# Copying four quadrants of a 256 MB matrix: DMAs of 64 rows from the four quadrants in turn, in place of DMAs of 512 rows

## Chip, cores and metric

One core of one Trainium2 chip. The metric is the device time of one execution in microseconds (us). Three calls of experiments follow the first comparison; each ran on one chip (the record numbers them 5, 15 and 5) and shares its own runs of the kernel before. Kernels are compared only within the same rounds.

## The reference

```python
def setup_inputs():
    return {"x": np.random.randn(8192, 8192).astype(np.float32)}

def reference(x):
    return np.fft.ifftshift(x)      # swaps the quadrants crosswise
```

With an even size this exchanges quadrants of 4096 x 4096: upper left with lower right, upper right with lower left. A row of a quadrant is 16 KB in one piece; the whole matrix has rows of 32 KB.

## The kernel before

No engine computes. SP (`nc.sync`) and ACT (`nc.scalar`) each issue 16 DMAs from main memory to main memory. A DMA takes every eighth row of one quadrant: 512 rows, 256 KB apart, 8 MB. The two queues always copy diagonal quadrants, so that reads and writes of left and right halves balance.

```python
STEP = 8
...
    dims = [[STEP * C, hr // STEP], [1, hc]]
    for c in range(STEP):
        for col in (0, hc):
            for eng, r0, h in ((nc.sync, 0, col), (nc.scalar, hr, hc - col)):
                eng.dma_start(
                    out=bass.AP(out.tensor, out.offset + (r0 + c) * C + h, dims),
                    in_=bass.AP(x.tensor, x.offset + (hr - r0 + c) * C + hc - h, dims),
                )
```

## Time and profile before

| | before |
|---|---|
| time, median of the 6 runs beside the change | 822.26 us (821.98 to 822.82) |
| copied | 268.4 MB, 327 GB/s |
| read and written in main memory | 654 GB/s |
| 16 KB packet: quickest (all but 22 of 16384 take at least this), median, mean | 611, 773, 801 ns |
| DMAs, completion writes (4 bytes each, by which an engine reports that its part of a DMA is done) | 32, 512 |

The prediction below shows the busy lines, the queues and the rate by stretch. One more view: how long the issuing instruction itself took. This is the view of the output tensor; the columns are least, median and longest duration in ns, then the first and last start in us.

```profile
L33 ACTq DMA_DIRECT2D out_dram<-in_x_dram x16: 518/42177/48098, 0.7 to 618.8; - x16
L33 SPq DMA_DIRECT2D out_dram<-in_x_dram x16: 511/41599/47782, 0.7 to 613.7; - x16
```

The shortest issue takes 0.51 us. The median of 42 us is not work. As I read it, the instruction stands until the queue has room for the last of its rows, while the engines work on the rows ahead of it; the trace does not name what it waits for. The engines' busy share is 1.00 meanwhile, so it costs nothing here.

### The profile page before, as it was taken

How to read it: one execution, taken by the hardware profiler on the slowest of the kernel's cores; microseconds unless marked ns; L12 is line 12 of the kernel's file. 1: busy time of each engine (PE TensorE's matmuls, PEld its weight loads, DVE VectorE, ACT ScalarE, POOL GpSimd, SP SyncE). 2: the span in 40 equal slices, each digit the busy share in tenths (PEclk: the TensorE clock that was granted, in tenths of full speed). 3: DMA queues.
4: the chain of work that ended last, by engine and by line, in shares of the span. 5: the costliest groups of instructions: out<-in, count | busy, mean ns of one | idle time of the engine just before them, and what ended most of it. 6: DMA issues, size and time to landing. Idle time of an engine off the chain costs nothing. (4 is left out here: it accounts for less than half of the span.)

```text
span 821.3 us, 77 instructions
## 1 busy us (share of the span) xinstructions
POOL 0.2 (0%) x4
## 2 busy tenths in 40 slices
POOL 0000000000000000000000000000000000000000
DMA  9999999999999999999999999999999999999998
GB/s 304 325 328 333 326 325 330 321 329 330 325 330 330 327 328 333 329 330 330 328 328 327 334 325 330 326 326 328 331 329 330 326 332 326 328 324 333 326 328 298
DMA packets 16896, 268.44 MB, mean 327 GB/s; under 512 B 512, under 2 KB 512, under 8 KB 512
## 3 DMA queue, kind: packets, MB, share of 16 engines
q1 hardware_dynamic: 8448, 134.22, 50.2%
q10 hardware_dynamic: 8448, 134.22, 49.7%
HBM read 268.44 MB, written 268.44 MB: 654 GB/s over the span
## 5 line engine op out<-in xcount | busy, mean ns | idle before, releaser
L51 POOL MEMSET const-bfloat16-1.0<- 128x1 bf16 x1 | 0.1, 103 | 0.0
L51 POOL MEMSET const-uint8-127<- 128x1 uint8 x1 | 0.1, 102 | 0.0
L51 POOL MEMSET const-float32-0.0<- 128x1 f32 x1 | 0.1, 99 | 0.2 <-issue 0.2
L51 POOL MEMSET const-float32-1.0<- 128x1 f32 x1 | 0.1, 99 | 0.0
## 6 DMA issues: line engine op xcount, KB each, us to landing
out_dram<-in_x_dram ACTq DMA_DIRECT2D x16, 8192.0 KB, 204.3
out_dram<-in_x_dram SPq DMA_DIRECT2D x16, 8192.0 KB, 204.1
```

What stands on the lines that cost most here:

```text
L51: nc = _bacc.Bacc("TRN2", target_bir_lowering=False, num_devices=1)
```

## The change

The change alters which rows are in flight at one time: shorter DMAs, engines closer together, and all four quadrants within a short time rather than two. Each DMA is cut to 64 rows (1 MB), and the second pair of quadrants changes queues, so that SP writes both left quadrants and ACT both right ones.

```diff
 STEP = 8
+PARTS = 8
...
-    dims = [[STEP * C, hr // STEP], [1, hc]]
+    n = hr // STEP // PARTS
+    dims = [[STEP * C, n], [1, hc]]
     for c in range(STEP):
-        for col in (0, hc):
-            for eng, r0, h in ((nc.sync, 0, col), (nc.scalar, hr, hc - col)):
+        for part in range(PARTS):
+            row = c + part * n * STEP
+            for eng, r0, h in (
+                (nc.sync, 0, 0),
+                (nc.scalar, hr, hc),
+                (nc.sync, hr, 0),
+                (nc.scalar, 0, hc),
+            ):
                 eng.dma_start(
-                    out=bass.AP(out.tensor, out.offset + (r0 + c) * C + h, dims),
-                    in_=bass.AP(x.tensor, x.offset + (hr - r0 + c) * C + hc - h, dims),
+                    out=bass.AP(out.tensor, out.offset + (r0 + row) * C + h, dims),
+                    in_=bass.AP(x.tensor, x.offset + (hr - r0 + row) * C + hc - h, dims),
                 )
```

## The prediction

> **What bounds the kernel now.** The program computes nothing: it copies four quadrants of 4096 x 4096 float32 (64 MB each) from one place in memory to another, so I started with the busy line of the whole span, then the queues, then the issues, then what the issuing engine waits for, and last the rate in separate stretches.
>
> The busy lines and the queues of the page (one digit is a fortieth of the span, GB/s is what was copied in it):
>
> ```profile
> DMA  9999999999999999999999999999999999999998
> GB/s 304 325 328 333 326 325 330 321 329 330 325 330 330 327 328 333 329 330 330 328 328 327 334 325 330 326 326 328 331 329 330 326 332 326 328 324 333 326 328 298
> DMA packets 16896, 268.44 MB, mean 327 GB/s; under 512 B 512, under 2 KB 512, under 8 KB 512
> ...
> q1 hardware_dynamic: 8448, 134.22, 50.2%
> q10 hardware_dynamic: 8448, 134.22, 49.7%
> HBM read 268.44 MB, written 268.44 MB: 654 GB/s over the span
> ```
>
> The 16 DMA engines are busy from start to end; only the first and last slices are lower. The two queues share them evenly (50.2% and 49.7%). 16896 packets are 16384 rows of 16 KB plus 512 tiny ones, which are the completion writes: 32 DMAs times 16 engines. A byte copied is read once and written once, so memory carries 654 GB/s.
>
> Is "busy" a full engine, or one that waits for memory? The packet records of the trace say: a 16 KB packet takes 611 ns at its quickest and about a quarter take that, the median is 773 ns, the mean 801 ns. 16384 B / 611 ns is 26.8 GB/s, times 16 engines 429 GB/s, which would be 268.44 MB / 429 = 626 us. The mean, 1024 packets per engine times 0.801 us = 820 us, is the whole span. So a packet is on average 31% slower than an engine can go, and what slows it is common to all. The 16 completion writes of each DMA land within 0.6 to 1.3 us of each other, even at its end: no engine is ahead of the rest. That fits one saturated common resource, memory, and not a slow engine or queue.
>
> Issues, and the issuing engine's waits:
>
> ```profile
> out_dram<-in_x_dram ACTq DMA_DIRECT2D x16, 8192.0 KB, 204.3
> out_dram<-in_x_dram SPq DMA_DIRECT2D x16, 8192.0 KB, 204.1
> ...
> SPq L62 <- DMA out_dram<-in_x_dram: 167.2, 2, 118.8
> SPq L33 <- DMA out_dram<-in_x_dram: 133.8, 12, 50.6
> ```
>
> A DMA of 8 MB at half of 327 GB/s takes 51.3 us; it lands 204 us after its issue, so four are in flight per queue. SP waits 12 times = 16 - 4: it may issue the next when the one four back has landed. This wait costs nothing, since three others are still queued.
>
> Last, the rate by stretch, each stretch holding one pair of DMAs or two:
>
> ```profile
> 2.00:53.00 51.00, 0.00 (x0) 1.00 1.00 329
> 53.00:104.00 51.00, 0.00 (x0) 1.00 1.00 329
> 104.00:155.00 51.00, 0.00 (x0) 1.00 1.01 328
> 155.00:206.00 51.00, 0.00 (x0) 1.00 1.01 326
> 206.00:308.00 102.00, 0.00 (x0) 1.00 1.00 328
> 410.00:512.00 102.00, 0.00 (x0) 1.00 1.00 328
> 614.00:716.00 102.00, 0.00 (x0) 1.00 1.01 329
> ```
>
> The last column is GB/s. It stays between 326 and 329 whichever row phase (one of eight) and column half is being copied. Sorting the packets by their place within a DMA (rows 0 to 31 of an engine, 256 KB apart) I also found no pattern beyond the scatter: even and odd rows both 798 to 805 ns. The rate does not care which of these address bits are set.
>
> **What the Trainium skill says.** (1) "HBM Reference", Specifications (TRN2): about 716 GB/s for the memory that two cores share, here used by one. The trace's 654 GB/s is 91% of it, with reads and writes mixed. (2) "DMA: Bandwidth & Descriptors", Issuing engines are not separate DMA queues: DMAs issued from several engines run on the same 16 DMA engines and interleave, so choosing who issues saves only issue time. The 50.2% and 49.7% agree. (3) Same page, section on why a DMA increments its semaphore by 16: a DMA is split over the largest k up to 16 that divides its slowest dimension, and each engine used ends with its own completion write. 512 tiny packets for 32 DMAs agree with k = 16; 64 rows also give 16, four rows each. (4) Same page, Latency and other measured facts, row on HBM row pitch at large powers of two: copies lose rate as the pitch grows, 207 GB/s at 512 KiB, 164 at 2 MiB, 103 at 4 MiB, against 214 padded; it calls the mechanism an inference. The trace before has 327 GB/s at a 256 KB pitch, so those sizes do not carry over.
>
> **The change, part by part.**
>
> Removed: nothing of the data. The same 16384 packets of 16 KB, same source and destination pairs, 1024 per engine. The floor of 626 us and memory's 537 MB stay.
>
> Added, issues: 256 DMAs in place of 32, 128 per queue. When the queue had room an issue took 0.51 to 0.62 us in the trace; 128 x 0.6 = 77 us per queue, beside 820 us of data. One DMA of 1 MB at 163.5 GB/s per queue takes 6.4 us, ten times its issue. Not on the path.
>
> Added, completion writes: 256 x 16 = 4096 in place of 512, so 224 more per engine. The records give 9 ns for each: 224 x 9 ns = 2.0 us. An upper figure: the trace has 8.7 us in which only 15 engines were busy; put wholly on the 512 writes that is 17 ns more each, so 224 x 26 ns = 5.8 us. Where memory is the limit, the other engines can use that gap, so I take +2 us.
>
> Changed, depth: four DMAs in flight per queue are now 4 MB rather than 32 MB, per engine 4 x 4 = 16 packets per queue. After a landing the next must be issued (0.6 us) and reach the engines: the first packet in the trace starts 1.4 us after its issue started. Meanwhile 3 x 6.4 = 19 us of work is queued. A gap needs engines to drift apart by some 12 packets of a queue; the trace shows 1.3 us at most, under two packets. Cost 0.
>
> Changed, order: rows handled at one time. If each engine takes consecutive rows (32 before, 4 after), engines were 32 x 256 KB = 8 MB apart and become 1 MB apart; a queue alternates between two quadrants each 6.4 us, not each 51 us. At any moment SP still copies one quadrant and ACT the diagonal one, so the mix of column halves read and written stays. The stretches above show no dependence on address bits from 16 KB (column half) up to 4 MB (row within an engine's share), so I expect little, but the bits which differ between engines change from 8 MB upward to 1 MB upward, and no record before tests that. I give it -4 us, with a wide spread.
>
> Changed, ends: the start (1.4 us to the first packet) is as before. q10 ends 2 us after q1 in the landings; finer DMAs may save about half, 1 us, lost in the rest.
>
> Sum: 822.3 + 2 (completions) + 0 (issue, depth) - 4 (order) = 820 us.
>
> **Rivals.**
>
> A. Memory conflicts fall, because engines no longer walk 8 MB apart. For: the skill's pitch table (if its engines hold eight rows each, 512 KiB is 4 MB between engines and 2 MiB is 16 MB, a loss of 3% and 23%, and 8 MB lies between); packets scatter from 611 to 1826 ns. Against: 654 is already 91% of 716 GB/s. Even all 716 would be 536.9 MB / 716 = 750 us; an estimate of 94%, 673 GB/s, gives 798 us. Time 790 to 805 us.
>
> B. Conflicts grow: four engines' rows now fall where one engine's fell, and each queue jumps between quadrants every four rows. For: the same table shows that pitch can matter a lot. Against: the flat stretches. 3 to 5% fewer GB/s would be 845 to 865 us.
>
> C. The shallow queue runs dry, because a new DMA waits for the slowest engine of the one four back. For: 124 such waits per queue in place of 12. Against: 19 us queued against 2 us of refill. If each wait leaked 0.2 us on both queues together it would be 25 us, 847 us; the DMA share would fall below 0.97.
>
> **Range and chances.** The known terms are worth +2 to +6 us, the end effects 1 us; all the width comes from A, B and C. A's limit is near, since memory is at 91%, so the lower end is 795; B or C of moderate size give the upper end, 848. 2% is 16.4 us: below 806 is faster, which needs 667 GB/s or more over the span, a rate that single slices reach (334 copied, 668 moved) but no 51 us stretch holds. I give it 0.22. Slower needs B or C at more than 16 us: 0.18. Same: 0.60.
>
> **What would show it.** Right: 20480 packets with 4096 under 512 B; some 25.6 us (4 x 6.4) from issue to landing; SP waiting 124 times, each under 7 us; DMA share 1.00 in the middle; 325 to 331 GB/s in every stretch; a mean packet near 800 ns. A would show the mean packet below 785 ns, with more packets at 611. B would show DMA share 1.00 and a mean packet above 815 ns. C would show a share below 1.00 with packets unchanged or quicker. The prediction is wrong if memory's rate depends on how far apart the engines' rows lie, the one thing the trace before cannot show.

## The result

The changed kernel takes 821.96 us (median of 6 runs, 821.5 to 822.85), before 822.26 us in the same rounds. The ratio is 0.9997, 95% interval 0.9984 to 1.001. Ratios here are the mean time of one kernel's runs over that of the other's of the same rounds, so not quite the ratio of the medians quoted.

The changed kernel's busy lines and queues, from its page:

```profile
DMA  9999999999999999999999999999999999999998
GB/s 302 328 328 331 327 328 329 328 325 331 329 328 329 330 329 331 323 331 332 326 325 329 327 329 323 328 331 326 331 331 327 335 323 333 331 331 327 327 328 295
DMA packets 20482, 268.47 MB, mean 327 GB/s; under 512 B 4096, under 2 KB 4096, under 8 KB 4096
...
q1 hardware_dynamic: 10240, 134.23, 50.1%
q10 hardware_dynamic: 10240, 134.23, 49.7%
...
HBM read 268.44 MB, written 268.44 MB: 654 GB/s over the span
```

The same rates as before, slice by slice, with eight times the completion writes. Two packets over the expected 20480 are instruction fetches.

Its issues, with the median us from issue to landing last, then what SP waited for (us in total, times, longest), then the issue durations in ns:

```profile
out_dram<-in_x_dram ACTq DMA_DIRECT2D x128, 1024.0 KB, 25.5
out_dram<-in_x_dram SPq DMA_DIRECT2D x128, 1024.0 KB, 25.5
```

```profile
SPq L40 <- DMA out_dram<-in_x_dram: 728.5, 124, 8.3
```

```profile
L40 SPq DMA_DIRECT2D out_dram<-in_x_dram x128: 511/511/832, 0.7 to 797.0; - x128
```

SP now waits 728 us in place of 134, in 124 places. Looked at alone this would be a serious finding, yet nothing became slower: the time moved from "the issue stands in a full queue" (42 us each, before) to "the issue waits for the DMA four back" (5.9 us on average). By that count the queue always held three more DMAs.

The changed kernel's rate by stretch, last column GB/s, to set against the same stretches in the prediction:

```profile
2.00:53.00 51.00, 0.00 (x0) 1.00 1.00 330
53.00:104.00 51.00, 0.00 (x0) 1.00 1.00 330
104.00:155.00 51.00, 0.00 (x0) 1.00 1.00 328
206.00:308.00 102.00, 0.00 (x0) 1.00 1.00 329
410.00:512.00 102.00, 0.00 (x0) 1.00 1.01 327
614.00:716.00 102.00, 0.00 (x0) 1.00 1.01 330
```

The packet records show where the small known cost went. Per engine, all 16 KB packets together took 820.3 us before and 816.2 us after, 4.0 us less (of the unrounded sums); the completion writes took 0.3 us before and 2.3 us after, 2.0 us more; and time in which an engine did nothing (from the number of packets under way at each moment, the first and last 10 us left out) went from 0.5 to 2.2 us. What the engines lost in one place the packets gained in another. That is what one expects if a shared limit sets the pace, and it is what the experiments test.

### The profile page after: what moved, and what is told of

Read it like the earlier page. It is cut to its first block, busy times and chain, and to the rows that moved or that the text cites. A ratio compares the mean times of both kernels' runs of the same rounds, so it can differ in the third digit from the quotient of the medians. Undisturbed runs are those within 1.5% of the kernel's fastest.

```text
span 820.7 us, 301 instructions
## 1 busy us (share of the span) xinstructions
POOL 0.2 (0%) x4
## 2 busy tenths in 40 slices
DMA packets 20482, 268.47 MB, mean 327 GB/s; under 512 B 4096, under 2 KB 4096, under 8 KB 4096
## 6 DMA issues: line engine op xcount, KB each, us to landing
out_dram<-in_x_dram ACTq DMA_DIRECT2D x128, 1024.0 KB, 25.5
out_dram<-in_x_dram SPq DMA_DIRECT2D x128, 1024.0 KB, 25.5
```

## The experiments

Theory M: one resource that all engines share is full, and it cares neither for the order of the rows, nor for their distance, nor for the number of DMAs. Rivals: X, the two halves of the change have effects that cancel; E, each engine is slowed by itself; A, memory conflicts depend on addresses and the two kernels happen to be alike; C, the queue runs dry; S, completion writes come on top. And what is the resource: H, main memory read and written together, or F, the way through the engines?

### order_only and size_only: the two halves of the change

`order_only` is the changed kernel with this edit:

```diff
-PARTS = 8
+    PARTS = 1
```

`size_only` is the changed kernel with the quadrants on the queues as before:

```diff
-                (nc.sync, hr, 0),
-                (nc.scalar, 0, hc),
+                (nc.sync, 0, hc),
+                (nc.scalar, hr, 0),
```

> Half of the change alone: DMAs of 512 rows as before, quadrants in turn as after (SP takes both left quadrants of the output, ACT both right ones). Theory M (one shared resource is full at 327 GB/s copied and does not care for the order): 822 us, within 0.3%. Rival X (two effects of the change that cancel): over 0.5% off, and size_only off by as much the other way.

> The other half alone: 64 rows per DMA as after, quadrants on the queues as before. Theory M: 822 to 824 us (224 more completion writes per engine, at most 2 us). Rival X: over 0.5% off and opposite to order_only.

Measured: 824.53 and 824.57 us, before on that chip 824.07 us; ratios 1.0001 (0.9986 to 1.0016) and 1.0005 (0.999 to 1.002). Neither half does anything, so nothing cancels: X falls. The distance between the engines belongs to size_only; order_only leaves it as before, since its DMAs keep their rows. That distance and completion writes do not cancel inside size_only is shown by apart1m_rows (that distance, no more writes) and rows16 (still more writes) below.

### engines15 and engines12: fewer DMA engines

The rows per DMA are chosen so that 15 or 12 is the largest number of engines that divides them; the remaining rows of each quadrant go in one last DMA on 16.

```diff
-    dims = [[STEP * C, hr // STEP], [1, hc]]
-    for c in range(STEP):
+    n = 492        # 12 engines; 510 for 15
+    main = [[STEP * C, n], [1, hc]]
+    rest = [[C, hr - STEP * n], [1, hc]]
+    for row, dims in [(c, main) for c in range(STEP)] + [(STEP * n, rest)]:
```

(and `c` becomes `row` in the two addresses)

> 510 rows per DMA, so 15 DMA engines carry it; the 16 rows left of each quadrant go in one DMA on 16. Theory M (a shared limit of 327 GB/s, engines can do 26.8 GB/s each, 15 of them 402): 267.4 MB / 327.5 GB/s = 816 us plus 3 us for the rest, 818 to 826 us, and the mean packet falls from 0.80 to about 0.75 us. Rival E (each engine is slowed by itself, 0.80 us per packet whatever the others do): 1088 packets x 0.801 us = 871 us plus 3, 875 us, the mean packet stays at 0.80 us.

> 492 rows per DMA, so 12 engines; the 160 rows left of each quadrant in one DMA on 16. Theory M: 12 engines at their quickest do 12 x 26.8 = 322 GB/s, so 257.9 MB in 802 us plus 32 us for the rest, 834 us as the least; near the shared limit some packets are still slowed: 834 to 900 us, mean packet of the 12 engines 0.61 to 0.67 us. Rival E: 1312 packets x 0.801 us = 1051 us plus 32, 1083 us.

Measured: engines12 835.6 us, ratio 1.0137 (1.0121 to 1.0154), about the least that was thought possible. A quarter of the engines is idle for 96% of the rows, and the copy is 1.4% slower. Its rate by stretch; the column before the last is the busy share of all 16 engines:

```profile
104.00:155.00 51.00, 0.00 (x0) 1.00 0.76 324
206.00:308.00 102.00, 0.00 (x0) 1.00 0.76 324
410.00:512.00 102.00, 0.00 (x0) 1.00 0.76 324
```

Twelve engines, share 0.76, move 324 GB/s where sixteen at share 1.00 move 328. In the packet records nearly all packets (98% of those between 100 and 700 us) take the quickest time, 611 ns; before, 26% do. So twelve engines copy main memory to main memory at their full 26.8 GB/s each: rival E, which asked for 1083 us, falls, and four further engines add only 1.4%, because then the mean packet takes 801 ns.

engines15 took 845.17 us, ratio 1.0271 (1.0236 to 1.0305). That is neither M's 818 to 826 us nor E's 875. Its stretches:

```profile
104.00:155.00 51.00, 0.00 (x0) 1.00 0.94 324
206.00:308.00 102.00, 0.00 (x0) 1.00 0.94 322
410.00:512.00 102.00, 0.00 (x0) 1.00 0.90 320
780.00:790.00 10.00, 0.00 (x0) 1.00 0.75 323
800.00:846.00 46.00, 0.00 (x0) 1.00 0.58 247
```

The mean packet fell as M says (738 ns over the whole run, 54% of them at 611 ns), and 15 busy engines (0.94 of 16) are far from their own limit of 402 GB/s. But the shared rate was 322, not 328 GB/s, worth 268.4 MB / 322 - 268.4 MB / 328 = 15 us, and some engines ran out of work before others, which shows as a share of 0.90 in the middle and 0.58 at the end.

The packet records show how. SP's first DMA was done at 44.4 to 45.3 us on three of its engines, and at 52.8 to 54.6 us on the other twelve (before: all sixteen within 1.3 us). The three ran ahead, as I read it until the limit on DMAs in flight held them up (share 0.90), and were done by 766 us. From 780 to 795 us the other twelve were at work and every packet took 611 ns, as in engines12. So the twelve had not been held back by a limit of their own, each engine's or a fixed group's: a common rate was divided unevenly, and they got more once others had finished. Why three of fifteen get their full pace, and why the common rate is 322 and not 328, stays open; M as stated, with one fixed rate, missed this run by 19 us.

### apart32k, apart1m_rows, same_half: which addresses are worked on together

`apart32k` and `apart1m_rows` are the kernel before with another way through the rows of a quadrant. The first dimension has 16 steps, one for each engine:

```diff
-    dims = [[STEP * C, hr // STEP], [1, hc]]
-    for c in range(STEP):
+    dims = [[1 * C, 16], [16 * C, 32], [1, hc]]      # apart32k
+    dims = [[32 * C, 16], [1 * C, 32], [1, hc]]      # apart1m_rows
+    for row in range(0, hr, 512):
```

(one of the two `dims` lines in each kernel, and again `c` becomes `row`)

`same_half` is the changed kernel with both queues on the same column half:

```diff
                 (nc.sync, 0, 0),
+                (nc.scalar, hr, 0),
+                (nc.sync, 0, hc),
                 (nc.scalar, hr, hc),
-                (nc.sync, hr, 0),
-                (nc.scalar, 0, hc),
```

> Before's order and 512 rows per DMA, but the 16 engines work on 16 neighbouring rows (32 KB apart) and each steps 512 KB from one of its rows to the next. Theory M (a shared limit that does not care for addresses): 822 us within 1%. Rival A (memory conflicts depend on how far apart the rows worked on together lie; 8 MB and 1 MB happen to be alike): over 2% off, either way.

> Before's order, 512 rows per DMA that follow one another: engines 1 MB apart as in the changed kernel, but each goes through neighbouring rows (32 KB apart) in place of every eighth. Theory M: 822 us within 1%. Rival A: over 2% off.

> 64 rows per DMA, but the two queues copy quadrants of the same column half: at any moment both read one half of the rows and write the other (before and after, the queues are on diagonal quadrants). Theory M: 822 us within 1%. Rival A, for the address bit of 16 KB: slower by over 2%.

This ran on another chip, where the kernel before takes 811.22 us. Measured: 811.89, 812.06 and 811.7 us; ratios 1.0006, 1.0001 and 1.0007, each with an interval of about 0.0015 either way. A falls for every distance tried: engines 32 KB or 1 MB apart, steps of 32 KB, 256 KB or 512 KB within an engine, balanced halves or all reads on one half. That the engines of the kernel before are 8 MB apart rests on the assumption that each takes consecutive rows of a DMA; no record names the engine, so the trace does not show it. With a first dimension of 16, as in these two kernels, the distance does not depend on that.

### rows16: 1024 DMAs of 16 rows

```diff
-    PARTS = 8
+    PARTS = 32
```

> The change taken further: 16 rows per DMA, one row per engine, 1024 DMAs of 256 KB; a completion write of 9 ns follows every 16 KB packet (1024 per engine, 992 more than before: 8.9 us of engine time), and only 4 packets per queue and engine are queued (4 x 1.6 us = 6.4 us, of which 4.8 us are left when one has landed). Theory M (the shared limit absorbs what the engines lose; the refill of some 2 us hides behind 4.8): 820 to 828 us, DMA share near 1. Rival C (queue runs dry, as each DMA waits for the slowest of 16 engines): over 840 us, share below 0.97. Rival S (completion writes come on top): 831 us or more with the share at 1.

Measured: 811.41 us, ratio 1.0004 (0.9989 to 1.0019). Its packets, its waits on SP and its issues:

```profile
DMA packets 32776, 268.57 MB, mean 332 GB/s; under 512 B 16384, under 2 KB 16384, under 8 KB 16384
```

```profile
SPq L41 <- DMA out_dram<-in_x_dram: 531.0, 500, 2.3
```

```profile
out_dram<-in_x_dram ACTq DMA_DIRECT2D x512, 256.0 KB, 6.3
out_dram<-in_x_dram SPq DMA_DIRECT2D x512, 256.0 KB, 6.3
```

One completion write now follows each 16 KB, and a DMA lands 6.3 us after its issue. Beside same_half on the same chip (64 rows per DMA), the packets of an engine take 797.5 us in place of 804.8, 7.3 us less, while its completion writes take 9.2 us in place of 2.3, 6.9 us more. S falls: the cost is real on the engine, and the shared limit absorbs it. C is not seen at this depth.

### loads_only and stores_only: what is full?

Their outputs are wrong, which doesn't matter for the times. All but 2 MB of the traffic in main memory goes one way. In place of the loops of the kernel before (the last line, which stores one tile, is left out here):

```diff
+    pool = ctx.enter_context(tc.tile_pool(name="p", bufs=8))
+    for b in range(R // 128):
+        for eng, h in ((nc.sync, 0), (nc.scalar, hc)):
+            t = pool.tile([128, hc], f32, name="t")
+            eng.dma_start(out=t, in_=x[b * 128:(b + 1) * 128, h:h + hc])     # loads_only
```

In `stores_only` one tile is loaded once, and the loop has `eng.dma_start(out=out[b * 128:(b + 1) * 128, h:h + hc], in_=t)`.

> Wrong on purpose: the same 268 MB are read in 16 KB rows, but into on-chip memory (2 MB per DMA, 128 rows), and almost nothing is written back. Engines move as many bytes, main memory sees half. Theory H (what is full is main memory, read and write together at some 655 GB/s): packets fall to their quickest time, 611 ns, 429 GB/s, about 626 to 640 us. Rival F (what is full is the way through the 16 engines, 327 GB/s of copied bytes whatever they go to): 811 to 824 us, packets at 0.80 us.

> Wrong on purpose: 268 MB are written to the output from one on-chip tile, almost nothing is read. Theory H: 626 to 640 us, packets at 611 ns. Rival F: 811 to 824 us. If reads run at 611 ns and writes do not, it is writing alone that is full.

Measured (on the chip of order_only and engines12, before 824.18 us): 639.48 and 641.85 us, ratios 0.776 and 0.7788. The lines of loads_only, then of stores_only:

```profile
GB/s 367 430 429 429 430 428 428 429 429 428 429 428 429 431 429 428 429 428 431 428 428 428 428 427 428 428 428 430 430 428 429 428 430 430 429 428 428 429 430 326
...
HBM read 268.44 MB, written 2.10 MB: 424 GB/s over the span
```

```profile
GB/s 328 426 426 426 426 426 426 426 426 426 426 426 426 426 426 426 426 426 426 426 426 431 426 427 426 426 428 426 426 427 426 429 426 426 426 426 426 428 428 377
...
HBM read 2.10 MB, written 268.44 MB: 423 GB/s over the span
```

Sixteen engines move 428 GB/s one way, packets at 615 ns in the median, which is the engines' own limit (16 x 26.8 = 429). F falls, and so does "writing alone is full". Together with engines12 this leaves H: the 654 GB/s of reading and writing in main memory at once is the limit. Whether it is the memory itself or the way to it that the engines share, no run tells apart.

### one_queue and rows16_one_queue: depth

`one_queue` is the changed kernel, `rows16_one_queue` is rows16, both with `nc.scalar` replaced by `nc.sync`.

> The changed kernel with all 256 DMAs issued by SP: 4 DMAs of 64 rows in flight in all, 16 packets per engine, 12.8 us of work. Theory M (shared limit; a queue is only a way to issue): within 0.5% of before. If two queues are needed to keep engines full: over 2% slower, share below 1.

> Depth cut to where it should hurt: 1024 DMAs of one row per engine, all on SP, 4 packets per engine in flight (3.2 us), each new DMA waiting for the slowest of 16 engines. Issue 0.51 us per 0.80 us. The first DMA of the changed kernel landed 6.5 us after issue, of which 4 packets of each of two queues at 0.61 us are 4.9, so some 1.6 us are latency; with one packet and 1 us of spread between engines a round takes about 3.2 us, just what is queued. If my account of depth (rival C) is right this is where gaps begin: 820 to 920 us with a DMA share of 0.88 to 0.98. If depth never matters: within 0.5% of before.

Measured: 824.77 and 824.73 us, ratios 1.0009 (0.9994 to 1.0024) and 1.0004 (0.9989 to 1.0019). A second queue is worth nothing here. But for rows16_one_queue I expected gaps, and the premise was wrong. Its lines:

```profile
q1 hardware_dynamic: 32768, 268.50, 99.7%
```

```profile
out_dram<-in_x_dram SPq DMA_DIRECT2D x1024, 256.0 KB, 6.4
```

A DMA of 256 KB takes 0.8 us at 327 GB/s, so 6.4 us to landing are eight in flight, not four. one_queue agrees: 25.6 us at 3.2 us each, and SP waits 248 times for its 256 DMAs:

```profile
SPq L41 <- DMA out_dram<-in_x_dram: 661.3, 248, 3.4
```

In every run the landings are counted on eight semaphores. The limit is eight DMAs in the whole program, shared by the queues that issue, so each kernel had as many packets per engine in flight as its two-queue version: 32 in one_queue, eight in rows16_one_queue. At that depth nothing is lost, although landings of one DMA on its 16 engines lie up to 3.1 us apart. A shallower queue was not tried, so the depth at which rival C begins stays open.

## Why the prediction was right, point by point

- **The bound.** "One saturated common resource, memory" held, and is now shown rather than argued: full-speed packets with 12 engines, full speed with 16 in one direction only, 327 GB/s when 16 engines both read and write main memory. Memory and the way to it are not told apart, and engines15 shows that the engines need not share it evenly.
- **Issues cost 0.** Right: 128 issues of 0.51 us per queue; even 1024 on one queue (0.51 us of every 0.80) changed nothing.
- **Completion writes cost +2 us.** The size on the engine was right (2.0 us), the sign in the sum was not: under a shared limit it adds 0, as rows16 shows with a 6.9 us increase absorbed. The prediction saw the reason and still added the term.
- **Depth costs 0.** Right for eight packets per engine and more. The prediction expected each wait under 7 us; the longest was 8.3 us.
- **Order gains 4 us.** Wrong in size: 0. The term was meant for the engines' distance, 8 MB to 1 MB, and for the quicker turn of quadrants; the distance is tested by size_only (1.0005) and alone by apart1m_rows (1.0001), the whole by the change (0.9997). order_only (1.0001) tests only which queue takes which quadrants. The two false terms, +2 and -4, nearly cancelled, so 820 us is near 821.96 partly by luck; the right sum is 822.3 + 0.
- **Rival A** took its support from the skill's pitch table. The flat stretches spoke against it and were the better witness: what the kernel's own trace shows outweighed a table of another shape. B, its mirror, falls with it.
- **Readings of the trace.** The prediction says that the rate stays between 326 and 329 GB/s, but it left out the stretch from 308 to 410 us, which had 331. First issues took up to 0.90 us, not 0.62. For "only 15 engines busy" I count again and find 7.2 to 7.6 us, not 8.7. Three per cent fewer GB/s is 848 us, not 845. None of these enters the sum.
- **The marks.** 4096 tiny packets, 25.5 us to landing (25.6 predicted), share 1.00, 327 to 330 GB/s, mean packet 797 ns: all as stated.

## What to carry to other kernels

When a busy engine's records show many packets above their quickest time, ask what the engines share before rearranging what they do: this copy, bound by its reads and writes in main memory together, did not react to DMA size, order, distance or queue within what was tried, and 6.9 us more of completion writes on each engine disappeared in it. Fewer engines are a cheap test of this: twelve of sixteen kept 98.6% of the speed. Look then at when each engine finishes, too: fifteen shared unevenly and lost more. SP's waits grew fivefold here and cost nothing, because work stayed queued behind them.

## What the Trainium skill lacked or had wrong

- "DMA: Bandwidth & Descriptors", Latency and other measured facts, the row on HBM row pitch: 207 GB/s at a pitch of 512 KiB against 214 padded, and far less beyond. Here copies of 16 KB rows with steps of 32 KB, 256 KB and 512 KB within an engine all copied 331 GB/s over the span on one chip (apart1m_rows, same_half, apart32k; in each direction, as the row counts), ratios 1.0001 to 1.0007. So the row's 207 GB/s is not what these copies get at that step, and no loss of 3% was seen. No run has the row's exact layout (the steps of 512 KB go with engines 32 KB apart); steps of 2 MiB and more, and padding, were not tried.
- "HBM Reference", Specifications (TRN2), gives one figure of 716 GB/s for the memory of a pair. The page does not state what a mix of reading and writing by one core reaches: with 16 engines 652 to 654 GB/s in the first comparison and on chip 5, and 662 to 663 on chip 15, for all the addresses tried.
- None of the pages read mentions that chips differ: the same kernel took 811.22 us on one and 822.26 to 824.18 us elsewhere, up to 1.6% more.
- "DMA: Bandwidth & Descriptors", Rules for kernel authors, asks for 1 MiB or more per DMA for bandwidth. With memory as the limit and eight DMAs in flight, 256 KB each lost nothing (rows16, 1.0004).
- None of them says that using 12 of 16 engines costs a memory-to-memory copy only 1.4%, and 15 of 16 more than that (2.7%).
